# Expert stage of a two-layer MoE block: wide and narrow quads of experts alternate, and the hidden transpose moves to another PSUM bank

## The chip, the cores and the metric

The kernel runs on one core of one Trainium2 chip. The metric is device time in microseconds of one execution, lower is better; the time before is the median of three runs. A profile of one further execution, with its own time, is the source of every duration below.

## What is computed

The program takes 256 tokens of width 1024 through two layers of a mixer block with a dense feed-forward part, and then through two layers that end in a mixture of experts. The change touches only the latter. Of the reference, what matters is this:

```python
D_MODEL, SEQ, DEPTH = 1024, 256, 2
N_GROUPS, EXPERTS_PER_GROUP, N_EXPERTS, TOP_K, D_EXPERT = 4, 8, 32, 2, 512

def hierarchical_moe(h, w_group, b_group, w_router, b_router, w_gate, w_up, w_down):
    g_logits = xf @ w_group + b_group          # a token picks one group of 8 experts
    e_logits = xf @ w_router + b_router        # and its two best experts in that group
    ...
    def expert_block(args):
        xblk, e = args
        hid = jax.nn.silu(xblk @ w_gate[e]) * (xblk @ w_up[e])
        return hid @ w_down[e]
    ...                                        # weighted sum of the two experts of each token
```

All in fp32. An expert's three matrices are 2 MB each, so a layer's 32 experts are 201 MB that are read from HBM once. With 256 tokens and two experts each, an expert has 16 tokens on the mean. Evaluating this routing on the reference's inputs gives the largest number of tokens of one expert in each of the eight consecutive groups of four experts: 34, 35, 30, 20, 22, 26, 30, 18 in layer 0 and 15, 19, 29, 28, 18, 20, 19, 16 in layer 1.

## The kernel before

The expert stage is the function `moe` (L1530). It works on **quads** of four experts, `qd` = 0 to 7. A token's place in an expert's list is its slot. In a **wide** quad each expert has 64 slots and the quad is done in two steps of two experts; in a **narrow** quad each has 32 slots and the quad is one step of four experts. In both cases a step fills the 128 columns of the TensorE array, 64 or 32 columns for each expert (`tile_position` at L1600 and L1628), and matmuls of different columns run beside each other. So TensorE needs about twice the time for a wide quad, while the weights to be loaded are the same. `steps(qd)` (L86) says which it is: before, quads 0 to 3 are wide and 4 to 7 narrow (`NWIDE = 4`).

A quad's work, by the names that the profile shows:

- `prep` (L1566) picks the tokens: one-hot matrices `sel` on DVE (L1538), then `gather` (L1544), 32 matmuls `xt` (L1554) into PSUM pool `pX` of two banks, and evictions `XT` by DVE (L1558) and ACT (L1560). The matmuls are 256 columns for a wide quad and 128 for a narrow one; a wide quad needs four banks, a narrow one two. There is one `XT` buffer, so evictions wait until the previous quad's gate and up products are done.
- `up` (L1590) makes the gate product `g` and the up product `u` (L1600), each in one PSUM bank of its own (`pG`, `pU`), then `sl` = silu(g)·u on ACT (L1607) and DVE (L1608).
- `hidden` (L1611) turns `sl` by four transposes `hTp` (L1614) into a bank of `pX` and copies it back on ACT (L1616).
- `down` (L1619) makes the down product `yp` (L1628), `halves` (L1633) scales and splits it, `combine` (L1642) adds it to `x` by 8 matmuls `cb` (L1648). `combine` of a step runs inside `up` of the next one, after the gate product was issued.

Weights come through a **ring** of 10 buffers of 1 MB (class `Ring`, L186; the stage's pools have 3, 4 and 3 of them). The loads stand in one list, are issued by SP in order (L220), and a load is issued when its buffer comes free, which is after the last matmul that read it. An expert needs 6 loads: two halves each of gate, up and down; a quad needs 24.

Before quad 6 (`XAT = 6`) stands a branch (`overflow`, L1692, taken at L1698) for experts whose tokens exceed their slots. Its condition is `rv > over`: the largest count in `key`, from which `cm` was subtracted (L1515 to L1518), so that narrow experts count from 33 tokens and wide ones from 65. After quad 5 the stage combines, passes the branch and only then prepares quad 6.

The order of instructions on each engine is made by a scheduler from the program and its buffers; it moves the matmuls of `gather` between those of other steps where the banks of `pX` allow.

Of the kernel before, what the change touches and what calls it, by code (L numbers as in the profile page):

```python
# [11 lines left out]
F32 = mybir.dt.float32  # L12
# [8 lines left out]
P = 128  # L21
# [37 lines left out]
NE = 32  # L59
DE = 512  # L60
QE = 4
NWIDE = 4
XCAP = 64
KEY = 64
ALPHA = (2.0 * DEPTH) ** 0.25
# [19 lines left out]

def steps(qd):  # L86
    e = QE * qd
    return [(e, 2, 64), (e + 2, 2, 64)] if qd < NWIDE else [(e, 4, 32)]


def const_layout():
# [162 lines left out]
def v3(a, b):  # L254
    return lambda t: t[:, : a * b].rearrange("p (a b) -> p a b", a=a)


class Kern:
# [862 lines left out]
    def plan_second(self, i):  # L1121
# [18 lines left out]
        for qd in range(NE // QE):  # L1140
            if qd == NE // QE - 1:
                ring.blank()
            for e0, n, w in steps(qd):
                es = range(e0, e0 + n)
                for nm in ("e_w_gate_2", "e_w_up_2"):
                    for hf in range(2):
                        for e in es:
                            ring.add((ap[nm][i, e].rearrange("(p k) f -> p k f", p=P)[:, 4 * hf : 4 * hf + 4, :], v3(4, DE)))
                for hf in range(2):
                    for e in es:  # L1150
                        ring.add((ap["e_w_down_2"][i, e].rearrange("(p f) d -> p f d", p=P)[:, 2 * hf : 2 * hf + 2, :], v3(2, D)))
# [294 lines left out]
    def route(self, i, pool, pC, rw, csum, crow, stats, meanwhile):  # L1446
        nc = self.nc
        tmp = pool.tile([P, DE], F32, name="rt", tag="sl")
        used = [0]

        def tt(w):
            used[0] += w
            return tmp[:, used[0] - w : used[0]]

        U32 = mybir.dt.uint32
        A = pool.tile([P, NT, NE], BF16, name="Am")
        R, W = [pool.tile([P, NT, NE], F32, name=n) for n in ("R", "W")]
        key, cm = [pool.tile([P, NE], F32, name=n) for n in ("key", "cm")]
        k8 = pool.tile([P, 8], F32, name="k8")
        mi = pool.tile([P, 4], I32, name="mi")  # L1460
        hT = [pool.tile([P, D], F32, name=n, tag=n).rearrange("p (q k s) -> p q k s", q=2, k=4) for n in ("XT", "y")]
        self.nmr, late = [], []
        for t, ((mu, rs), bs) in enumerate(stats):
            for q, b in enumerate(bs):
                if EV[2 * t + q] == "v":
                    nc.vector.tensor_copy(hT[t][:, q], b)
                else:
                    with self.after(*([self.sq_last] if EV[2 * t + q] == "b" else [])):
                        nc.scalar.copy(hT[t][:, q], b)
            lg = pC.tile([P, 36], F32, name="lg", tag="c")  # L1470
            for k in range(KT):
                last = nc.tensor.matmul(lg, lhsT=hT[t][:, k // 4, k % 4, :], rhs=rw[:, k, :], start=k == 0, stop=k == KT - 1)
            nm = pool.tile([P, 1], F32, name="nmr", tag="nmr", bufs=2)
            self.nmr.append(nm)
            L = tt(36)
            nc.vector.tensor_tensor(nm, mu, rs, ALU.mult)
            nc.vector.scalar_tensor_tensor(L, csum, nm, crow, ALU.mult, ALU.add)
            nc.vector.scalar_tensor_tensor(L, lg, rs, L, ALU.mult, ALU.add)
            G, E = L[:, 0:4], L[:, 4:36]
            gm, t4, ix, ml, m8, xf, o1 = tt(1), tt(4), tt(1), tt(NE), tt(8), tt(2), tt(NE)  # L1480
            x8 = tt(8).bitcast(U32)
            nc.vector.tensor_reduce(gm, G, axis=AX.X, op=ALU.max)
            nc.vector.scalar_tensor_tensor(t4, G, gm, self.c("rev4"), ALU.is_equal, ALU.mult)
            nc.vector.tensor_reduce(ix, t4, axis=AX.X, op=ALU.max)
            nc.vector.tensor_scalar(t4, t4, ix, -1.0, op0=ALU.is_equal, op1=ALU.add)
            nc.vector.scalar_tensor_tensor(
                ml.rearrange("p (g e) -> p g e", g=4), t4.unsqueeze(2).to_broadcast([P, 4, 8]), -NEG,
                E.rearrange("p (g e) -> p g e", g=4), ALU.mult, ALU.add,
            )
            nc.vector.max(m8, ml)  # L1490
            nc.vector.max_index(x8, m8, ml)
            nc.vector.tensor_scalar(xf, x8[:, 0:2], -1.0, 32.0, op0=ALU.mult, op1=ALU.add)
            nc.vector.tensor_scalar(o1, self.c("rev32"), xf[:, 0:1], None, op0=ALU.is_equal)
            nc.vector.scalar_tensor_tensor(A[:, t, :], self.c("rev32"), xf[:, 1:2], o1, ALU.is_equal, ALU.add)
            late.append((G, gm, ml, m8, xf, t4))
        with self.after(last):
            meanwhile()
        rk = pC.tile([P, 3, NE], F32, name="rk", tag="c")
        nc.tensor.matmul(rk[:, 0, :], lhsT=self.strictb, rhs=A[:, 0, :], start=True, stop=False)
        nc.tensor.matmul(rk[:, 1:3, :], lhsT=self.onesb, rhs=A[:, 0, :].unsqueeze(1).to_broadcast([P, 2, NE]), start=False, stop=False)  # L1500
        nc.tensor.matmul(rk[:, 2, :], lhsT=self.onesb, rhs=A[:, 1, :], start=False, stop=False)
        nc.tensor.matmul(rk[:, 1, :], lhsT=self.strictb, rhs=A[:, 1, :], start=False, stop=True)
        r_last = nc.vector.scalar_tensor_tensor(R, rk[:, 0:2, :], 1.0, A, ALU.add, ALU.mult)

        def weights():
            for t, (G, gm, ml, m8, xf, t4) in enumerate(late):
                nc.vector.tensor_scalar(xf[:, 0:1], m8[:, 0:1], -1.0, None, op0=ALU.mult)
                nc.vector.tensor_scalar(xf[:, 1:2], gm, -1.0, None, op0=ALU.mult)
                nc.scalar.activation(ml, ml, AF.Exp, bias=xf[:, 0:1])
                nc.scalar.activation(t4, G, AF.Exp, bias=xf[:, 1:2], accum_out=gm)  # L1510
                nc.scalar.activation(m8[:, 1:2], m8[:, 1:2], AF.Exp, bias=xf[:, 0:1])
                nc.vector.scalar_tensor_tensor(gm, m8[:, 1:2], 1.0, gm, ALU.add, ALU.mult)
                nc.vector.reciprocal(gm, gm)
                nc.vector.scalar_tensor_tensor(W[:, t, :], ml, gm, A[:, t, :], ALU.mult, ALU.mult)
            nc.vector.memset(cm[:, : QE * NWIDE], 0.0)  # L1515
            nc.vector.memset(cm[:, QE * NWIDE :], float(32 - XCAP))
            nc.vector.tensor_tensor(key, rk[:, 2, :], cm, ALU.subtract)
            nc.vector.scalar_tensor_tensor(key, key, float(KEY), self.c("rev32"), ALU.mult, ALU.add)  # L1518
            nc.vector.max(k8, key)
            nc.vector.max_index(x8, k8, key)  # L1520
            nc.vector.tensor_copy(mi[:, 0:2], x8[:, 0:2])
            nc.vector.scalar_tensor_tensor(gx, k8[:, 0:1], float(-KEY * XCAP), k8[:, 2:3], ALU.add, ALU.max)
            nc.vector.tensor_copy(mi[:, 2:3], k8[:, 0:1])
            nc.vector.tensor_copy(mi[:, 3:4], gx)

        x8 = tt(8).bitcast(U32)
        gx = tt(1)
        return R, W, (key, cm, k8, mi), weights

    def moe(self, i, pool, A, B, R, W, g1, xs, weights, late, pG, pU, pY, pX, pC):  # L1530
        nc = self.nc
# [34 lines left out]
        def prep(qd, then=None):  # L1566
            w = steps(qd)[0][2]
            sel = slots(QE * w)
            last = pick(sel, QE, w, R, slice(QE * qd, QE * qd + QE))
            if then:  # L1570
                with self.after(last):
                    then()
            return gather(sel), sel
# [35 lines left out]
            return sl, last  # L1609

        def hidden(sl):  # L1611
            b = pX.tile([P, 4, P], F32, name="hTp", tag="x")
            for f in range(4):
                nc.tensor.transpose(b[:, f, :], sl[:, f::4], self.ident)  # L1614
            hid = v3(4, P)(sl)
            nc.scalar.copy(hid, b)  # L1616
            return hid
# [401 lines left out]
```

## Time and profile before

| | |
|---|---|
| median of 3 runs | 2090.56 us (2088.88 to 2095.25) |
| the profiled execution's own time | 2082.7 us |
| its span | 2080.5 us |
| TensorE busy, share of the span | 1869.5 us, 90% |
| mean DMA rate over the span | 288 GB/s |
| expert stage of layer 0, first gate matmul to last down matmul | 984.7 to 1455.2 us |
| expert stage of layer 1, likewise | 1591.7 to 2064.3 us |

A busy TensorE in these rows is not one at its peak, because matmuls overlap and their ends are modelled. The DMA share is the mean busy share of 16 DMA engines, and in the expert stage GB/s tells directly how fast weights arrive: 422 to 423 GB/s is the most that any longer stretch shows. PEclk is the granted TensorE clock, 1.00 being 2.4 GHz and 0.50 being 1.2 GHz.

### The profile page before, as it was taken

The numbers are of one execution on the slowest core, as the hardware profiler recorded it, in microseconds if no ns is written. First come the engines' busy times: TensorE is split into PE (matmuls) and PEld (weight loads), VectorE is DVE, ScalarE is ACT, GpSimd is POOL, SyncE is SP. The second block draws the span as 40 slices with busy tenths as digits, with TensorE's granted clock in tenths as the row PEclk, the third lists the DMA queues.
The fourth block names the chain that finished last, engine by engine and source line by source line (L and its number), as shares of the span: only waits on it lengthen the run. The fifth ranks groups of instructions, "written<-read, shape, count | busy, mean of one in ns | idle before, by whom it ended". The sixth has DMA issues, their size and how long they took to land. (4 is left out here: it accounts for less than half of the span.)

```text
span 2080.5 us, 27466 instructions
## 1 busy us (share of the span) xinstructions
PE 1869.5 (90%) x10924; PEld 1252.4 (60%) x10924; DVE 985.7 (47%) x1979; ACT 600.5 (29%) x1158; POOL 183.7 (9%) x219
## 2 busy tenths in 40 slices
PE   7999999999989999688999997687898999987775
PEld 7887899998879998666444432231895443331321
DVE  6556779574667786986222121110884222211112
ACT  5434534273445442324111110010443111010010
POOL 2210000021100001620200000000330200000000
PEclk9787999996889998798999999889898999999898
DMA  7232879451349796355899989999755999989996
GB/s 217 88 102 81 317 259 370 152 156 60 102 169 322 273 351 212 119 169 206 362 423 422 422 322 424 421 390 416 255 196 229 423 422 422 390 339 422 413 400 266
DMA packets 178252, 598.51 MB, mean 288 GB/s; under 512 B 19008, under 2 KB 105408, under 8 KB 128960
## 3 DMA queue, kind: packets, MB, share of 16 engines
q1 hardware_dynamic: 174912, 592.47, 74.3%
q10 hardware_dynamic: 1872, 2.26, 0.3%
q0 software_dynamic: 1328, 1.90, 0.3%
q8 instruction: 90, 1.47, 0.3%
q14 instruction: 50, 0.41, 0.1%
HBM read 594.66 MB, written 1.93 MB: 287 GB/s over the span
## 5 line engine op out<-in xcount | busy, mean ns | idle before, releaser
L378 DVE TENSOR_TENSOR wlo<-w,whi 128x1024 fp32r<-128x1024 f32 (+3 forms) x232 | 280.6, 1222 | 102.2 <-ACT whi L377 101.2
L377 ACT CAST whi<-w 128x1024 fp32r<-128x1024 f32 (+3 forms) x232 | 224.2, 983 | 229.0 <-PE gu L412 60.9
L1600 PE MATMUL g<-w,XT 128*64 128x512 f32 (+1 forms) x1024 | 240.4, 631 | 17.7 <-DMA w<-in_e_w_gate_dram 17.7
L1628 PE MATMUL yp<-w,sl 128*64 128x512 f32 (+1 forms) x1024 | 237.3, 631 | 17.8 <-DMA w<-in_e_w_down_dram 10.7
L1600 PE MATMUL u<-w,XT 128*64 128x512 f32 (+1 forms) x1024 | 215.3, 615 | 28.5 <-DMA w<-in_e_w_up_dram 28.5
L1638 DVE SCALAR_TENSOR_TENSOR y<-yp,ws,g 128x512 f32<-128x512 f32 x48 | 35.9, 749 | 293.7 <-PE yp L1628 286.9
L1608 DVE TENSOR_TENSOR sl<-sl,u 128x512 f32<-128x512 f32 x24 | 16.5, 687 | 312.6 <-PE u L1600 312.6
L1628 PEld LDWEIGHTS yp<-w,sl 128*64 128x64 f32 (+1 forms) x1024 | 69.9, 129 | 157.1 <-issue 113.2
L1600 PEld LDWEIGHTS u<-w,XT 128*64 128x64 f32 (+1 forms) x1024 | 61.8, 126 | 157.9 <-issue 108.7
L413 PE MATMUL gu<-hTf,wlo 128*128 128x256 f32 x512 | 147.0, 287 | 0.7 <-DVE wlo L378 0.6
L411 PE MATMUL gu<-hTf,whi 128*128 128x256 f32 x512 | 146.7, 287 | 0.8 <-ACT whi L377 0.8
L412 PE MATMUL gu<-hTf,whi 128*128 128x256 f32 x512 | 146.4, 286 | 0.0
L1600 PEld LDWEIGHTS g<-w,XT 128*64 128x64 f32 (+1 forms) x1024 | 63.0, 129 | 136.4 <-issue 100.6
L813 DVE SCALAR_TENSOR_TENSOR aacc<-w,ca,aacc 128x1024 f32<-128x1024 f32 x84 | 107.5, 1280 | 2.0 <-DMA w<-in_ada_w_dram 1.4
L399 ACT CAST yh<-y 128x512 fp32r<-128x512 f32 x48 | 29.7, 618 | 259.0 <-DVE y L1638 259.0
L411 PEld LDWEIGHTS gu<-hTf,whi 128*128 128x128 f32 x512 | 98.8, 193 | 2.7 <-ACT whi L377 1.0
L412 PEld LDWEIGHTS gu<-hTf,whi 128*128 128x128 f32 x512 | 99.4, 194 | 1.4
L413 PEld LDWEIGHTS gu<-hTf,wlo 128*128 128x128 f32 x512 | 98.7, 193 | 2.4 <-DVE wlo L378 1.1
L1554 PE MATMUL xt<-sel,nhh 128*128 128x256 f32 (+1 forms) x256 | 77.1, 328 | 22.5 <-DVE sel L1538 15.4
L1654 DVE TENSOR_TENSOR x<-x,cb 128x512 f32<-128x512 f32 x88 | 58.1, 685 | 79.5 <-PE cb L1648 79.3
L411 PE MATMUL mm<-whi,hT 128*128 128x384 f32 (+2 forms) x256 | 89.0, 355 | 4.6 <-ACT hT L495 4.6
L412 PE MATMUL mm<-wlo,hT 128*128 128x384 f32 (+2 forms) x256 | 89.8, 354 | 0.0
(476 smaller groups left out, 3697.8 us busy)
## 6 DMA issues: line engine op xcount, KB each, us to landing
w<-in_e_w_gate_dram SPq DMA_DIRECT2D x128, 1024.0 KB, 13.0
w<-in_e_w_down_dram SPq DMA_DIRECT2D x128, 1024.0 KB, 14.7
w<-in_e_w_up_dram SPq DMA_DIRECT2D x128, 1024.0 KB, 13.9
w<-in_ada_w_dram SPq DMA_DIRECT2D x48, 1024.0 KB, 7.7
w<-in_w_gate_dram SPq DMA_DIRECT2D x22, 1024.0 KB, 6.7
w<-in_w_up_dram SPq DMA_DIRECT2D x22, 1024.0 KB, 7.5
w<-in_w_down_dram SPq DMA_DIRECT2D x22, 1024.0 KB, 6.5
w<-in_w_in_dram SPq DMA_DIRECT2D x16, 768.0 KB, 4.4
```

The source lines that it names most:

```text
L377: self.half_act = nc.scalar.copy(hi, src)
L378: self.half_last = nc.vector.tensor_tensor(lo, src, hi.bitcast(F32), ALU.subtract)
L399: a = nc.scalar.copy(hi, src)
L411: nc.tensor.matmul(out, lhsT=a[0], rhs=b[0], start=start, stop=False)
L412: nc.tensor.matmul(out, lhsT=a[0], rhs=b[1], start=False, stop=False)
L413: self.mm_last = nc.tensor.matmul(out, lhsT=a[1], rhs=b[0], start=False, stop=stop)
L813: nc.vector.scalar_tensor_tensor(acc, w[:, j, :], c, acc, ALU.mult, ALU.add)
L1554: nc.tensor.matmul(b[:, k, :], lhsT=nh[hl][:, t, c0 : c0 + P], rhs=sel[:, t, :], start=t + hl == 0, stop=t + hl == NT)
L1600: last = nc.tensor.matmul(ps[c, :], lhsT=XT[:, kk, c], rhs=wt[j][:, k, :], start=kk == 0, stop=kk == KT - 1, tile_position=(0, w * j))
L1628: nc.tensor.matmul(ps[h][c, :], lhsT=hid[:, ff + f, c], rhs=wt[j][:, f, h * 512 : (h + 1) * 512], start=ff + f == 0, stop=ff + f == 3, til ...
L1638: nc.vector.scalar_tensor_tensor(y[:, c], ps[h], ws, g1[:, c], ALU.mult, ALU.mult)
L1654: nc.vector.tensor_tensor(a, a, b, ALU.add)
```

## The change

Quads 0, 1, 3 and 5 are wide now, and 2, 4, 6 and 7 narrow; there are four of each as before. `cm` is set by five memsets for two. The hidden transpose `hTp` takes the bank of the up product (`pU`, one bank) in place of one of the two of `pX`; the up product has been read by then, since `sl` is its last reader.

```diff
-NWIDE = 4
+WIDE = (0, 1, 3, 5)
...
 def steps(qd):
     e = QE * qd
-    return [(e, 2, 64), (e + 2, 2, 64)] if qd < NWIDE else [(e, 4, 32)]
+    return [(e, 2, 64), (e + 2, 2, 64)] if qd in WIDE else [(e, 4, 32)]
...
-            nc.vector.memset(cm[:, : QE * NWIDE], 0.0)
-            nc.vector.memset(cm[:, QE * NWIDE :], float(32 - XCAP))
+            nc.vector.memset(cm, float(32 - XCAP))
+            for qd in WIDE:
+                nc.vector.memset(cm[:, QE * qd : QE * qd + QE], 0.0)
...
         def hidden(sl):
-            b = pX.tile([P, 4, P], F32, name="hTp", tag="x")
+            b = pU.tile([P, 4, P], F32, name="hTp", tag="u")
```

In the changed program every line from L1516 on stands one lower, so `xt` is L1555, `hTp` L1615, `yp` L1629. How many gather matmuls `xt` the scheduler puts into each quad of a layer (from that quad's first `hTp` up to the next quad's): before, 32, 32, 32 and 64 in the wide quads 0 to 3 and none in the narrow quads 4 and 5; with the change 40 and 30 in quads 0 and 1, 48 in the narrow quad 2, 16 in the wide quad 3, 16 in the narrow quad 4 and none in the wide quad 5. The rest of quad 0's comes ahead of its first `hTp`.

TensorE before, second step of the wide quad 3 in layer 0 (`yp` is the down product, `w` the loaded weights; rows of the same kind are left out):

```order
L1614 MATMUL hTp<-ident,sl 128x128 x4
L1554 MATMUL xt<-sel,nhh 128x128
...
L1628 MATMUL yp_10888<-w_10685,sl 64x512
L1628 MATMUL yp_10888<-w_10687,sl 64x512
...
L1554 MATMUL xt<-sel,nhl 128x128
L1628 MATMUL yp_10888<-w_10699,sl 64x512
...
L1600 MATMUL g<-w_10731,XT 32x512
```

All 32 gather matmuls for quad 5 stand here, 16 between the transposes and the down product, 6 inside it and 10 after the next quad's first gate matmul.

TensorE with the change, the first step of the wide quad 3 in layer 0:

```order
L1615 MATMUL hTp<-ident,sl 128x128 x4
L1629 MATMUL yp_10677<-w_10550,sl 64x512
L1629 MATMUL yp_10678<-w_10550,sl 64x512
L1629 MATMUL yp_10677<-w_10552,sl 64x512
...
L1649 MATMUL cb<-yh,C 128x512
L1601 MATMUL g<-w_10574,XT 64x512
```

No gather stands in this step any more. Those for quads 3 and 4 have gone to the narrow quad 2, whose down product reads:

```order
L1615 MATMUL hTp<-ident,sl 128x128 x4
L1555 MATMUL xt<-sel,nhh 128x256
...
L1629 MATMUL yp_10532<-w_10363,sl 32x512
...
L1555 MATMUL xt<-sel,nhl 128x256
L1629 MATMUL yp_10532<-w_10367,sl 32x512
...
L1555 MATMUL xt<-sel,nhh 128x128
L1629 MATMUL yp_10532<-w_10369,sl 32x512
```

Here 48 gather matmuls stand between the 32 down matmuls.

ACT at the end of quad 3, before (`XT` is the gather's eviction, L1616 the copy that ends the use of the `hTp` bank):

```order
L1607 ACTIVATE sl<-g 128x512
L1560 ACTIVATE XT<-xt,B,A 128x128 x4
L1616 COPY sl<-hTp 128x512
L399 CAST yh<-y 128x512 x2
```

and with the change:

```order
L1608 ACTIVATE sl<-g 128x512
L1561 ACTIVATE XT<-xt,B,A 128x128 x2
L1617 COPY sl<-hTp 128x512
L1561 ACTIVATE XT<-xt,B,A 128x128 x2
```

The copy no longer stands behind all four evictions.

## Rows read from the trace of the kernel before

**Rows 1.** Page, parts 1 and 2: busy time; DMA share in 40 slices.

```profile
PE 1869.5 (90%) x10924; PEld 1252.4 (60%) x10924; DVE 985.7 (47%) x1979; ACT 600.5 (29%) x1158; POOL 183.7 (9%) x219
...
DMA  7232879451349796355899989999755999989996
```

**Rows 2.** Windows: length, busy by engine, PEclk, DMA share, GB/s.

```profile
1103.27:1195.00 91.73, 87.30 (x408) 36.73 (x406) 19.70 (x32) 9.98 (x21) 0.00 (x0) 0.98 1.01 422
1195.00:1255.00 60.00, 56.77 (x303) 21.86 (x303) 13.31 (x23) 6.74 (x15) 0.00 (x0) 0.94 0.85 336
1255.00:1345.00 90.00, 62.98 (x324) 18.75 (x314) 14.43 (x26) 6.28 (x13) 0.00 (x0) 0.90 1.01 423
1345.00:1375.00 30.00, 30.00 (x203) 15.34 (x205) 1.64 (x4) 2.86 (x7) 0.00 (x0) 0.80 0.91 364
...
1770.00:1865.00 95.00, 90.94 (x476) 36.16 (x476) 19.36 (x32) 9.58 (x21) 0.00 (x0) 0.98 0.91 358
...
1955.00:1985.00 30.00, 29.48 (x208) 15.28 (x207) 1.96 (x5) 2.86 (x7) 0.00 (x0) 0.84 0.90 364
```

**Rows 3.** DMA view, gate loads issued in 1110-1165, 1165-1245 and 1271-1330: us to landing.

```profile
w<-in_e_w_gate_dram SPq DMA_DIRECT2D x8, 1024.0 KB, 12.6
...
w<-in_e_w_gate_dram SPq DMA_DIRECT2D x8, 1024.0 KB, 7.4
...
w<-in_e_w_gate_dram SPq DMA_DIRECT2D x8, 1024.0 KB, 19.7
```

**Rows 4.** Waits of SP's queue, 1200 to 1255: us in total, times, longest.

```profile
SPq L220 <- PE g L1600: 22.7, 6, 9.5
SPq L220 <- PE yp L1628: 16.8, 3, 11.7
```

**Rows 5.** Groups by line, PE, quads 2 and 3 (1103.27 to 1235.12), and that window.

```profile
L1554 PE MATMUL xt<-sel,nhh 128*128 128x128 f32 (+1 forms) x43 | 12.3, 317 | 2.0 <-ACT XT L1560 2.0
L1554 PE MATMUL xt<-sel,nhl 128*128 128x128 f32 (+1 forms) x43 | 12.0, 309 | 0.0
...
L1614 PE MATMUL hTp<-ident,sl 128*128 128x128 f32 x16 | 3.3, 337 | 3.7 <-ACT XT L1560 2.7 <-DVE sl L1608 1.0
...
1103.27:1235.12 131.85, 124.50 (x557) 51.38 (x554) 28.39 (x48) 15.07 (x32) 0.00 (x0) 0.96 0.98 403
```

**Rows 6.** Timeline of PE at the end of quad 3 [idle before].

```profile
1209.65 7.04 PE L1600 MATMUL u<-w,XT 128*64 128x512 f32 x30
1219.35 0.75 PE L1614 MATMUL hTp<-ident,sl 128*128 128x128 f32 x4 [2.66 <-ACT XT L1560]
...
1222.68 6.04 PE L1628 MATMUL yp<-w,sl 128*64 128x512 f32 x16
...
1231.47 3.65 PE L1628 MATMUL yp<-w,sl 128*64 128x512 f32 x12
```

**Rows 7.** Windows of PE alone there: busy, PEclk, DMA share, GB/s.

```profile
1215.00:1220.00 5.00, 2.34 (x12) 1.00 1.01 426
1220.00:1225.00 5.00, 5.00 (x23) 0.57 1.02 428
1225.00:1230.00 5.00, 5.00 (x16) 0.75 0.24 85
```

**Rows 8.** Groups by line, PE, narrow quad 5 (1271.46 to 1331.96), and that window.

```profile
L1628 PE MATMUL yp<-w,sl 128*32 128x512 f32 x67 | 16.3, 600 | 3.0 <-DMA w<-in_e_w_down_dram 2.3 <-ACT sl L1616 0.7
L1600 PE MATMUL g<-w,XT 128*32 128x512 f32 x64 | 14.7, 732 | 3.3 <-DMA w<-in_e_w_gate_dram 3.3
L1600 PE MATMUL u<-w,XT 128*32 128x512 f32 x64 | 13.2, 642 | 6.2 <-DMA w<-in_e_w_up_dram 6.2
...
1271.46:1331.96 60.50, 45.90 (x226) 11.87 (x224) 6.36 (x11) 3.47 (x7) 0.00 (x0) 0.92 1.01 422
```

**Rows 9.** Waits of SP's queue at the branch, 1348 to 1369.

```profile
SPq L1698 <- SPq L1698: 19.4, 6, 5.3
```

**Rows 10.** Source view of L1515: one memset of `cm`, ns min/median/max.

```profile
L1515 DVE MEMSET cm<- x2: 72/72/72, 981.4 to 1588.4; 128x16 f32 x2
```

## The prediction

> **What bounds the kernel now.** I read the page first. TensorE is busy for 90% of the span and DMA is at nine tenths in most slices of the last half [rows 1], so the page alone doesn't say which of the two bounds the expert stage. The windows do. DMA moves 422 or 423 GB/s through nearly the whole stage: in quads 2 and 3 of layer 0 up to 1195 us, and again from 1255 us [rows 2]. That is the ceiling, since TensorE waits for loads in the second of these stretches and still gets no more [rows 8]. A quad is 24 loads of 1024 KB [rows 3], 25.17 MB, and takes 25.17 / 0.422 = 59.6 us at that rate. So the stage is bound by the loads, and time can be won only where DMA stops.
>
> It stops at two places in a layer. One is between 1195 and 1255 us, at 336 GB/s, which is where quad 3, the last wide one, hands over to quad 4; in layer 1 the like stretch is 1770 to 1865 us, at 358 GB/s [rows 2]. The other is at the branch after quad 5, 364 GB/s in 30 us in both layers [rows 2].
>
> Why the first? A load is issued when a ring buffer is free, so the time from issue to landing tells how many loads are queued; 10 buffers at 2.48 us each (59.6 / 24) make 24.8 us. For gate loads it is 12.6 us in quad 2's stretch, 7.4 us from 1165 us on, and 19.7 us in the narrow quad 5 [rows 3]. So the queue shrinks while wide quads run: TensorE frees buffers more slowly than DMA fills them, until DMA stops. What SP then waits for is TensorE, 22.7 us for gate and 16.8 us for down matmuls [rows 4]. TensorE's pace in quads 2 and 3 is 131.85 / 2 = 65.9 us a quad [rows 5] against 59.6. In quad 5 it has 45.9 us of busy time, waits for all three products' loads, and DMA is full [rows 8].
>
> **The change, part by part.** *The order of the quads.* The same four wide and four narrow quads run, so neither bytes nor matmuls change; what moves is the gather. Before, quad 3 alone has 64 gather matmuls and quads 4 and 5 have none. Now the wide quad 3 has 16, the wide quad 5 none and the narrow quad 2 has 48. In the two quads of rows 5 the gather's groups are busy for 12.3 + 12.0 = 24.3 us, and TensorE stands 2.0 us before `xt` and 2.7 us before `hTp`, each for evictions of `XT`. Without them the two quads are 131.85 - 29.0 = 102.9 us, 51.4 us a quad. I give quads 3 and 5 between 51.4 us and, with 16 gather matmuls at 24.3 / 86 = 0.28 us, 55.9 us. Both are under 59.6 us. Quads 0 and 1 keep their place and about their gather (70 matmuls for 64, some narrower), so they leave the queue as they did, at 12 us or more. Then the narrow quad 2 fills it up, quad 3 no longer empties it, and quad 4 and quad 5 repeat that. The stop at the hand-over goes: (422 - 336) / 422 x 60.00 = 12.2 us in layer 0 and (422 - 358) / 422 x 95.00 = 14.4 us in layer 1, **26.6 us** together. Since loads bound the rest of the stage, the end of it comes that much earlier, and what follows each stage hangs on its end.
>
> *The gather in quad 2.* 48 matmuls at 0.28 us are 13.4 us, put between down matmuls that are busy for 16.3 us [rows 8]. Together they are 29.7 us, where the eight down loads take 19.9. Quad 2 then ends up to 9.8 us late. Its cover is the queue: 24.8 us less the 7.4 us from issue to landing at which it ran dry, 17.4 us. So I cost it at nothing; with that cover gone, at 9.8 us a layer.
>
> *The transpose's bank.* Before, `hTp` at the end of quad 3 stood 2.66 us for the evictions, and the granted clock of the next windows was 0.57 and 0.75; 16 down matmuls there took 6.04 us, and 12 a little later 3.65 [rows 6, 7]. In `pU` it waits for `sl` only, and the copy no longer stands behind four evictions. That gain is in the 2.7 us above, and I don't count it twice. What is late next: the next up product needs the bank back. a whole gate product stands ahead of it on TensorE, so the copy is done by then, and I cost it at nothing; if it were not, TensorE would wait before every up product, and the loads' queue would cover that as well.
>
> *The branch.* SP stands 19.4 us at the branch [rows 9], for all loads in flight to land, before it issues another. That doesn't depend on the quads' widths, so (422 - 364) / 422 x 30.00 = 4.1 us a layer stays. If TensorE reached it far later, more would be lost; by the sum above quad 5 ends where its loads do, as now.
>
> *The memsets.* Three more, at 72 ns [rows 10], 0.2 us a layer if nothing hides them, in work that DVE does just ahead of the first gate matmul. 26.6 - 0.4 = 26.2; I take **26.5** off, with no more precision meant than 2 us.
>
> The profiled execution took 2082.7 us, so the sum gives 2056. The median of the runs shown is 2090.56, 8 us above it, and I forecast a median: 2090.56 - 26.5 = **2064 us**.
>
> **Rivals.** *Quad 2's gather is not absorbed* (place: its down product). For it: 29.7 us of TensorE work on 19.9 us of loads, and quads 0 and 1 may leave TensorE behind already. Against: 17.4 us of cover. Price 9.8 us a layer, 19.6 in all: 2064 + 19.6 = **2084 us**.
>
> *The hand-over itself stops DMA*, since a narrow step needs four experts' halves at once and keeps four buffers until all are used. For it: the stop in both layers lies just there, and SP waits for gate matmuls there [rows 4]. Against: the time from issue to landing fell through quad 3 already [rows 3]. There are now two more hand-overs ahead of quad 6, from quad 1 to 2 and from 5 to 6, and the branch hides the second. If only the one in the middle still costs, nothing is won: 2090 us; if that from quad 1 to 2 costs as much, 26.6 us more: 2117 us.
>
> *The clock falls in wide quads that wait for loads.* This is the rival on the other side. Wide quads now have gaps before loads as quad 5 had. At a granted clock of 0.50, 51.4 us at 0.96 become 98.7 us, 39.1 over the loads' 59.6; 17.4 of it the queue covers, and 21.7 are lost in each of quads 3 and 5, so 43.4 a layer against some 13.3 won: 30 us a layer slower, **2151 us**. It decides where two quads lose 13.3 us together, at an overrun of 24 us: a mean clock of 51.4 x 0.96 / 83.6 = 0.59. Against: quad 5, with waits before all three products, was granted 0.92 [rows 8], and at 0.92 a wide quad is 53.6 us.
>
> The Trainium skill, TensorE: Matmul & The Clock Gate, section "Why this matters for your kernels", speaks against the change: it wants the matmuls dense, and has a loop that waits for a transfer before each burst of matmuls run with the cold clock. By that rule the time would be this last rival's 2151 us. Rows 7 agree that the clock falls behind a stall; rows 8 show that waits of this kind before loads cost little of it.
>
> That a narrow quad's experts overflow, so that the branch is taken, is excluded: quads 2 and 4 have at most 30 and 22 tokens an expert.
>
> **How the numbers follow.** About 0.3%, 6.3 us, is what a measurement of this kernel can tell from no change. Forecast 78%: 2058 to 2072. Gather not absorbed, wholly or in part, 12%: up to 2084. Hand-over 6%, of it 4% without change and 2% slower. Clock 4%. So faster 0.90, same 0.04, slower 0.06. The range goes down to 2054: all 26.6 us, half of the 8.2 us at the branches, and the 6 us by which runs differ; and up to 2084, the first rival. Outside lie the 10% of the other two.
>
> **What would show it.** Right: in both layers 422 GB/s from the first freed buffers to the branch, with no dip where a wide quad ends; gate loads of quads 3 and 5 with about 19 us from issue to landing; TensorE waiting for loads inside wide quads; no wait of `hTp` for `XT`; the branch's 364 GB/s dip as it was. Wrong: a dip in quad 2 or 3 (gather), dips at quad 1 to 2 and 3 to 4 (hand-over), a clock under 0.8 in quads 3 and 5 (clock), or a full DMA rate with the end of the stage where it was.

## The result and the profile after

The changed kernel takes **2066.6 us**, the median of 4 runs (2065.01 to 2067.24). The kernel before takes 2089.72 beside it (2087.91 to 2095.25, 4 runs). The ratio is 0.9884 with a 95% interval of 0.9864 to 0.9904: the change made the kernel 23.1 us, 1.2%, faster. The forecast was 2064 us, with a range of 2054 to 2084.

The profiled execution of the changed kernel took 2067.24 us, with a span of 2065.0. First the page, parts 1 and 2, which answers to [rows 1]:

```profile
PE 1876.1 (91%) x10924; PEld 1251.1 (61%) x10924; DVE 981.7 (48%) x1985; ACT 599.7 (29%) x1158; POOL 186.5 (9%) x219
...
DMA  6232879552339798337699999999755999999996
```

TensorE has the same number of instructions and 6.6 us more busy time, in a span that is 15.5 us shorter. The digits of the DMA row show where the change is. In the kernel before, an 8 stood in each expert stage past its first slice, in those that begin at 1196 and 1820 us. Now every slice that lies wholly in one of the two stages is a 9.

The windows of the changed kernel (columns as in [rows 2]): quads 2, 3, 4 and 5 of layer 0, each from the last down matmul of the quad ahead to its own last one, then the branch of each layer.

```profile
1108.05:1149.99 41.94, 40.35 (x288) 17.88 (x288) 8.63 (x15) 4.89 (x10) 0.00 (x0) 1.00 1.01 422
1149.99:1214.63 64.64, 59.52 (x254) 22.53 (x254) 14.27 (x24) 7.12 (x17) 0.00 (x0) 0.97 1.01 423
1214.63:1266.67 52.04, 42.43 (x240) 12.70 (x240) 8.23 (x14) 5.50 (x11) 0.00 (x0) 0.93 1.01 422
1266.67:1327.49 60.82, 55.56 (x237) 20.27 (x236) 11.92 (x18) 5.61 (x12) 0.00 (x0) 1.00 1.01 423
1345.00:1375.00 30.00, 28.29 (x200) 13.40 (x199) 3.71 (x9) 4.09 (x11) 0.00 (x0) 0.88 0.89 359
...
1940.00:1970.00 30.00, 30.00 (x205) 14.92 (x205) 1.64 (x4) 2.86 (x7) 0.00 (x0) 0.84 0.90 362
```

DMA is at 422 or 423 GB/s in all four quads, where [rows 2] had 336 at the hand-over. The dip at the branch is as it was. The lengths tell why: the narrow quad 2 takes TensorE 41.94 us and the narrow quad 4 52.04, where the loads of a quad take 59.6. The wide quad 3 takes 64.64 and the wide quad 5 60.82. A wide quad falls behind the loads by 1 to 5 us, and the narrow one ahead of it has given more than that.

What SP waits for says the same. First the kernel before, in the wide quads 2 and 3 (1110 to 1195 us), then the changed kernel in quads 3 to 5 (1150 to 1330 us): us in total, times, longest.

```profile
SPq L220 <- PE yp L1628: 31.1, 6, 9.6
SPq L220 <- PE g L1600: 23.7, 9, 5.5
SPq L220 <- PE u L1600: 17.8, 8, 4.1
```

```profile
SPq L220 <- DMA w<-in_e_w_up_dram: 51.6, 24, 3.3
SPq L220 <- DMA w<-in_e_w_gate_dram: 50.0, 24, 2.1
SPq L220 <- DMA w<-in_e_w_down_dram: 49.7, 24, 2.1
SPq L220 <- PE yp L1629: 1.2, 4, 0.4
```

Before, SP waited for TensorE to free a buffer. Now it waits for other loads to land, 72 times, and for TensorE for next to nothing. The last four gate loads of quad 3 and the eight of quad 4, issued from 1146 to 1205 us, have 19.7 us to landing where the wide quads of [rows 3] had 12.6 and 7.4:

```profile
w<-in_e_w_gate_dram SPq DMA_DIRECT2D x12, 1024.0 KB, 19.7
```

**An account by landings.** Each load's record has the time at which it landed. A layer has 192 expert loads, counted here in the order in which they land, of 2.48 us each at the full rate, so a stretch can be told by how much later than that its loads land. I give three numbers a layer. A: from the first gate matmul to the landing of the 48th load, the last of quad 1. B: by how much the 96 loads of quads 2 to 5 land later than 238.1 us after it. C: by how much the last 48, with the branch, land later than 119.0 us after those. The sum with 238.1 and 119.0 is the stage from its first gate matmul to its last load. Layers 0 and 1, in us, from the profiled execution of each kernel:

| kernel | A | B | C | stage | median, us |
|---|---|---|---|---|---|
| before | 92.4, 92.9 | 13.1, 14.9 | 4.2, 4.1 | 466.8, 469.0 | 2089.7 |
| changed | 94.2, 95.5 | 1.2, 1.1 | 3.8, 4.1 | 456.3, 457.8 | 2066.6 |

The stages are 10.5 and 11.2 us shorter, 21.7 together. B gives 11.9 + 13.8 = 25.7, A takes 1.8 + 2.6 = 4.4 of it back, and C gives 0.4. The two profiled executions differ by less, 15.5 us, because that of the changed kernel began its first gate matmul 5.6 us later (990.3 for 984.7), after code that the change doesn't touch. Three executions of the changed kernel have this start at 984.0, 986.0 and 990.3, so executions differ by that much in any case.

### The profile page after: what moved, and what is told of

The parts are those of the page before. It is cut to its first block, busy times and chain, and to the rows that moved or that the text cites. A ratio compares the mean times of both kernels' runs of the same rounds, so it can differ in the third digit from the quotient of the medians.

```text
span 2065.0 us, 27481 instructions
## 1 busy us (share of the span) xinstructions
PE 1876.1 (91%) x10924; PEld 1251.1 (61%) x10924; DVE 981.7 (48%) x1985; ACT 599.7 (29%) x1158; POOL 186.5 (9%) x219
## 5 line engine op out<-in xcount | busy, mean ns | idle before, releaser
L378 DVE TENSOR_TENSOR wlo<-w,whi 128x1024 fp32r<-128x1024 f32 (+3 forms) x232 | 274.4, 1195 | 102.1 <-ACT whi L377 101.2
L1629 PE MATMUL yp<-w,sl 128*64 128x512 f32 (+1 forms) x1024 | 230.3, 599 | 19.2 <-DMA w<-in_e_w_down_dram 9.9
L1601 PE MATMUL u<-w,XT 128*64 128x512 f32 (+1 forms) x1024 | 221.0, 627 | 28.6 <-DMA w<-in_e_w_up_dram 28.5
L1601 PE MATMUL g<-w,XT 128*64 128x512 f32 (+1 forms) x1024 | 230.1, 630 | 8.5 <-DMA w<-in_e_w_gate_dram 8.5
L1629 PEld LDWEIGHTS yp<-w,sl 128*64 128x64 f32 (+1 forms) x1024 | 67.0, 123 | 149.5 <-issue 107.6
L399 ACT CAST yh<-y 128x512 fp32r<-128x512 f32 x48 | 29.7, 618 | 238.7 <-DVE y L1639 238.7
L1561 ACT ACTIVATE XT<-xt,B,A 128x256 f32<-128x256 f32 (+1 forms) x64 | 31.6, 515 | 206.8 <-DVE XT L1559 206.8
## 6 DMA issues: line engine op xcount, KB each, us to landing
w<-in_e_w_gate_dram SPq DMA_DIRECT2D x128, 1024.0 KB, 19.7
w<-in_e_w_up_dram SPq DMA_DIRECT2D x128, 1024.0 KB, 19.7
```

The lines of the kernel that those rows point to most:

```text
L378: self.half_last = nc.vector.tensor_tensor(lo, src, hi.bitcast(F32), ALU.subtract)
L399: a = nc.scalar.copy(hi, src)
L1561: nc.scalar.activation(XT[:, kk, :], b[:, k, :], AF.Identity, scale=A[:, kk : kk + 1], bias=B[:, kk : kk + 1])
L1601: last = nc.tensor.matmul(ps[c, :], lhsT=XT[:, kk, c], rhs=wt[j][:, k, :], start=kk == 0, stop=kk == KT - 1, tile_position=(0, w * j))
L1629: nc.tensor.matmul(ps[h][c, :], lhsT=hid[:, ff + f, c], rhs=wt[j][:, f, h * 512 : (h + 1) * 512], start=ff + f == 0, stop=ff + f == 3, til ...
```

## The experiments

**Theory.** The order wins: the narrow quads 2 and 4 fill the queue of loads before a wide quad draws on it, and nothing else counts. The bank costs a little in quads 0 and 1. **Rivals:** the bank wins, by taking the transposes off the evictions; or it is the hand-over, or strict alternation, that decides.

### The order alone, twice

```diff
-            b = pU.tile([P, 4, P], F32, name="hTp", tag="u")
+            b = pX.tile([P, 4, P], F32, name="hTp", tag="x")
```

> The changed kernel with the order of the quads alone: hTp stays in the xt bank. Theory (the order wins by keeping loads queued through quads 2 to 5; the bank only costs a little in quads 0 and 1, where the second step's up product now stands behind the first step's transposes): the middle of the stage loads without a stop as in the changed kernel, and the late landings of quads 0 and 1, 4.0 and 5.0 us a layer in the changed kernel, go back to about 2 us: 2062 us (2059 to 2066). Rival (the bank is what wins, the order follows along): no more than a third of the gain, 2082 us or above, with the stop near the end of quad 3 still there. Rival (both needed): some 2070 to 2076, with hTp waiting for XT's evictions in narrow quads.

Measured: **2063.83 us** (before beside it 2090.87; ratio 0.988, 0.986 to 0.99). A 92.8, 92.9; B 1.3, 1.1; C 4.2, 4.2. All of the gain in B is there without the bank, and A is back at what it was before the change. The rival that the bank wins falls, and with it the one that needs both: `hTp` still waits for evictions of `XT` here, 5.6 us in three places from 1093 to 1333 us, and the loads of quads 2 to 5 land as in the changed kernel.

This run also tells the order from the gather's new place. Without the bank the scheduler leaves most of the gather on the wide quad 3. Quads 2 and 3 of layer 0, cut as above, and then the gather's `xt` alone in quad 3 (busy time of PE, PEld, DVE and ACT, with no column for POOL):

```profile
1109.05:1145.63 36.58, 33.68 (x248) 13.62 (x248) 8.37 (x15) 4.61 (x10) 0.00 (x0) 0.95 1.01 422
1145.63:1215.60 69.97, 65.50 (x287) 26.79 (x288) 14.25 (x24) 7.60 (x17) 0.00 (x0) 0.98 1.01 423
...
1145.63:1215.60 69.97, 7.73 (x48) 6.71 (x48) 1.48 (x4) 1.61 (x4) 0.98 1.01 423
```

Quad 3 has 48 gather matmuls and takes 69.97 us, 10 more than its loads, and DMA stays at 423 GB/s. The narrow quad 2 ahead of it took 36.58, 23 less than its loads. So it is the narrow quad ahead of it that wins, and not that the gather has left quad 3, as it has in the changed kernel.

> The kernel with the order of the quads alone once more, now beside the changed kernel on the same chip. Theory (the bank costs 2 to 3 us a layer in quads 0 and 1 and gives nothing back): loads of quads 0 and 1 late by 2 us a layer, those of quads 2 to 5 by 1 to 2, and a median 4 us under the changed kernel's. Rival (the bank's cost there is taken back in quads 2 to 5): the same median within 1 us.

Measured: 2067.29 us (ratio 0.9883, 0.9865 to 0.9901), A 92.2, 92.9, B 1.6, 1.1. The landings agree with the theory again. The median doesn't: it lies 1.5 us above that of the changed kernel beside it, and the theory wanted 4 below.

### The bank alone

```diff
-WIDE = (0, 1, 3, 5)
+WIDE = (0, 1, 2, 3)
```

> The kernel before with hTp in the up product's bank alone: quads 0 to 3 wide, then 4 narrow. Theory (order wins): the stop at the hand-over stays for the most part; the wait of hTp for XT (2.7 us in two quads of layer 0) goes, and quads 0 and 1 lose 2 to 3 us a layer of landings: between 2084 and 2092 us. Rival (the bank wins): 2066 to 2072 us, no stop between 1195 and 1255 us.

Measured: **2095.5 us**, ratio to before 1.002 (1.0006 to 1.0033), so slower, and 3.5 us above the range that I gave. A 94.2, 94.9; B 12.9, 16.7. The windows of quads 2 to 5, from 100 us after the first gate matmul of each layer, for the bank alone (columns as in [rows 2]):

```profile
1091.65:1331.65 240.00, 211.87 (x1071) 79.42 (x1070) 48.16 (x81) 24.96 (x55) 0.00 (x0) 1.00 0.98 400
1703.91:1943.91 240.00, 215.43 (x1072) 80.14 (x1072) 48.96 (x82) 25.73 (x57) 0.00 (x0) 0.98 0.97 395
```

And the like windows of the changed kernel:

```profile
1090.34:1330.34 240.00, 217.31 (x1101) 81.10 (x1100) 51.73 (x87) 26.39 (x57) 0.00 (x0) 0.98 1.01 423
1686.90:1926.90 240.00, 217.96 (x1116) 81.36 (x1113) 51.36 (x87) 27.60 (x59) 0.00 (x0) 0.99 1.01 421
```

400 and 395 GB/s against 423 and 421, and 401 and 397 in the like windows of the kernel before: with the bank and the old order the stop stays whole. That `hTp` no longer waits for `XT` won nothing, although that wait was in the trace before.

### The changed kernel again, twice

> The changed kernel itself, unchanged, beside the other kernels of this call on the same chip. Both theories: 2066 to 2069 us. If it comes out at 2071 us or above, the 2073 and 2072 us of the kernels with wide quads 0, 1, 4, 5 and with 0, 1 alone lie within what this chip's executions differ by, and nothing is to be read from their medians against 2066.6 us.

Measured: 2068.71 us (2061.21 to 2075.35), A 94.0, 95.0, B 1.4, 1.2. That is under the 2071 us that I had set, so this run doesn't put the 2073 and 2072 us of the two kernels below down to scatter.

> The changed kernel once more, as the measure for the other three of this call: loads of quads 0 and 1 late by 4 to 5 us a layer by the theory; by the rival that the first two measurements of this stretch were chance, anything between 2 and 5.

Measured: 2065.76 us, A 94.2, 95.1, B 1.3, 1.4. In three executions A is 94.0 to 95.5 with the bank. In the two with the order alone and in that of before it is 92.2 to 92.9. The bank's cost in quads 0 and 1 is no chance, though its 17th to 48th loads are late by 3.5 to 5.0 us, a little less than I wrote.

### Where wide quads follow one another

Two in a row, after two narrow ones:

```diff
-WIDE = (0, 1, 3, 5)
+WIDE = (0, 1, 4, 5)
```

> Wide quads 0, 1, 4, 5: two wide ones in a row after two narrow ones, nothing else changed. Theory (what counts is that the queue is full when wide quads begin, and that TensorE's lag over two of them stays under the 17 us of cover): no stop, 2066 us (2064 to 2069), issue to landing of gate loads falls in quad 5 from 20 to 8-14 us. Rival (wide and narrow must alternate; the pair itself stops DMA as quads 2 and 3 did): a stop of some 5 to 13 us a layer near quad 5's end, 2076 to 2090 us.

Measured: 2073.19 us (2069.66 to 2075.85; ratio to before 0.9918, 0.9903 to 0.9934). A 94.8, 95.2; B 1.1, 2.5; C 4.0, 5.0; stage 457.1, 459.9. There is no stop near quad 5's end, so the rival of strict alternation falls. Half of my expectation fell too: the time to landing didn't sink in quad 5, where it is 19.9 us. Quads 4 and 5, in this kernel both wide:

```profile
1205.70:1268.09 62.39, 57.95 (x254) 22.38 (x254) 14.20 (x22) 7.76 (x17) 0.00 (x0) 1.00 1.01 422
1268.09:1326.19 58.10, 53.87 (x237) 21.10 (x234) 12.09 (x18) 6.22 (x13) 0.00 (x0) 1.00 1.01 423
```

With 16 gather matmuls in it a wide quad falls behind by 2.8 us; the next one, with none ahead of the branch, wins 1.5 back. So a wide quad draws the queue down by what gather it has: in the profiles of all the kernels here the wide quads from 2 on took 56.3 to 61.1 us without any, and 66.2 to 71.6 with 36 or more, in layers 0 and 1. Before, quads 2 and 3 had 32 and 54 in each layer, cut the same way, and nothing narrow between them. The median is 6.6 us above the changed kernel's first one, and the stages account for 2.9 of that.

Three in a row, from the start:

```diff
-WIDE = (0, 1, 3, 5)
+WIDE = (0, 1, 2, 5)
```

> Wide quads 0, 1, 2, 5 instead of 0, 1, 3, 5: three wide ones in a row at the start, then two narrow ones. Theory (the queue is drawn down quad by quad while wide quads follow one another from the start, and DMA stops once it is gone): two in a row stopped nothing in the changed kernel and four in a row cost 13 to 17 us a layer in the kernel with the bank alone, so three leave a stop of 2 to 6 us a layer, ahead of the narrow quad 3: 2070 to 2078 us. Rival (one hand-over costs the same wherever it lies): 9 us or more a layer there, 2085 us or above. Rival (only the fourth wide quad in a row does harm): none, 2067 us.

Measured: **2084.74 us** (2070.97 to 2087.37; ratio to before 0.9959, 0.9941 to 0.9977). A 94.2, 95.4; B 6.9, 7.6; C 4.6, 4.6. The stop lies in the loads of quad 3, as the theory has it, but is 7 us a layer where I gave 2 to 6, and the median lies 6.7 us above my range. The time is near the rival's 2085, but that rival wants a like stop at the first hand-over of the changed kernel, from quad 1 to 2, and its 24 loads after that land 0.2 us early and 0.3 late. Two wide quads from the start cost nothing, three 7 us a layer, four 13 to 17. What SP waits for there, 1135 to 1190 us, is TensorE again:

```profile
SPq L220 <- PE yp L1629: 23.6, 6, 8.2
SPq L220 <- PE g L1601: 10.9, 3, 6.6
SPq L220 <- PE u L1601: 5.5, 3, 2.6
```

Only quads 0 and 1 wide:

```diff
-WIDE = (0, 1, 3, 5)
+WIDE = (0, 1)
```

> Only quads 0 and 1 wide, the other six narrow: the same loads, less TensorE work from quad 2 on. Theory (from quad 2 on the changed kernel is bound by the loads alone): the same time as the changed kernel, 2066 us (2063 to 2068). Rival (wide quads 3 and 5 still cost something by themselves, in TensorE's time or clock): 2055 to 2061 us.

Measured: 2072.44 us (2067.56 to 2077.32; ratio to before 0.9918, 0.9898 to 0.9937), and 2067.56 in the profiled execution, 0.3 above the changed kernel's. A 94.2, 94.5; B 1.5, 2.6; stage 457.0, 459.0. With two wide quads fewer the stage is no shorter. So quads 3 and 5 cost nothing in the changed kernel by being wide, and what bounds it from quad 2 on is the loads. The median misses my range by 4 us; the stages account for 1.9.

### The branch taken away

```diff
-                self.overflow(i, pool, A, B, R, W, g1, xs, pG, pU, pY, pX, pC, (pick, gather, slots, turn, up, hidden, down, halves, combine))
```

> The changed kernel without the branch for overflowing experts ahead of quad 6, so that this path is left out; the gather for quad 6 stays where it is. Theory (the loads bound the stage, and SP's drain ahead of the branch costs them 4 us a layer): 8 us less than the changed kernel, 2058 us (2056 to 2061), and the loads of quads 6 and 7 land within 0.5 us of the full rate. Rival (what stood behind the branch is lost anyway, in TensorE's gather ahead of quad 6): less than 3 us, 2064 us or above.

Measured: **2058.99 us** (2051.1 to 2063.92; ratio to before 0.984, 0.9812 to 0.9868), 9.7 below the changed kernel beside it. C is 0.0, 1.3 for 3.8, 4.1; the stages are 452.4, 455.1, so 3.9 and 2.7 shorter. The window with quad 6's start in each layer shows no dip:

```profile
1330.00:1375.00 45.00, 39.48 (x217) 12.22 (x219) 8.13 (x17) 4.26 (x10) 0.00 (x0) 0.92 1.01 423
1930.00:1975.00 45.00, 37.78 (x207) 11.41 (x209) 7.45 (x13) 4.26 (x10) 0.00 (x0) 0.89 1.01 423
```

The price of the branch, 4.1 us a layer, was read rightly from its dip, though layer 1 gave a little less than that back: its last 48 loads are 1.3 us late where I gave 0.5.

### What the bank does in quads 0 and 1

The bank only from quad 2 on:

```diff
-        def hidden(sl):
-            b = pU.tile([P, 4, P], F32, name="hTp", tag="u")
+        def hidden(sl, own=False):
+            b = pX.tile([P, 4, P], F32, name="hTp", tag="x") if own else pU.tile([P, 4, P], F32, name="hTp", tag="u")
...
-                pend = (C, halves(down(hidden(sl), n, w, take, self.ring.done), ws))
+                pend = (C, halves(down(hidden(sl, qd < 2), n, w, take, self.ring.done), ws))
```

> The changed kernel with hTp in the xt bank for quads 0 and 1 and in the up product's bank from quad 2 on. Theory (the up product's bank costs 2 to 3 us a layer in quads 0 and 1 and nothing later): the late landings of quads 0 and 1 go from 4.0 and 5.0 back to 2 us, 4 to 5 us less than the changed kernel beside it, like the kernel with the order alone: 2062 to 2064 us. Rival (the bank costs in quads 2 to 5 too, or not at all): as the changed kernel, 2066 to 2068 us, or with late landings from quad 2 on.

Measured: 2069.12 us (ratio to before 0.9894, 0.987 to 0.9918). A 92.5, 93.1; B 1.4, 1.3; stage 455.2, 455.5. By the landings the theory holds: A is back and nothing is lost later. By the median it can't be told from the changed kernel beside it, 2068.71, and it lies 5 us above the range that I gave.

What changes there stands in TensorE's timeline. The second step of quad 0, in the kernel before (start, us, instruction):

```profile
1012.75 2.31 PE L1600 MATMUL u<-w,XT 128*64 128x512 f32 x9
...
1015.61 7.07 PE L1628 MATMUL yp<-w,sl 128*64 128x512 f32 x32
1022.51 5.32 PE L1600 MATMUL u<-w,XT 128*64 128x512 f32 x22
```

And in the changed kernel:

```profile
1021.99 7.07 PE L1629 MATMUL yp<-w,sl 128*64 128x512 f32 x32
1028.88 5.31 PE L1601 MATMUL u<-w,XT 128*64 128x512 f32 x22
1034.12 0.51 PE L1649 MATMUL cb<-yh,C 128*128 128x512 f32 x1
```

Before, 10 up matmuls of the second step ran ahead of the first step's down product. The first two up buffers are read by 16, so they came free soon after it: the two loads that waited for them were issued 38.9 and 39.7 us after the first gate matmul. Now all of them stand behind the down product, and those two loads are issued at 42.2 and 42.6. Also, 10 matmuls of quad 1's gather stand ahead of the first step's transposes now. In the 100 us from the first gate matmul, what SP waits for shifts. Before:

```profile
SPq L220 <- PE g L1600: 47.2, 11, 13.1
SPq L220 <- PE yp L1628: 18.2, 6, 4.9
SPq L220 <- PE u L1600: 12.7, 10, 3.0
```

In the changed kernel:

```profile
SPq L220 <- PE g L1601: 36.7, 13, 8.5
SPq L220 <- PE yp L1629: 25.8, 7, 11.4
SPq L220 <- PE u L1601: 19.5, 11, 4.1
```

To tell the shared bank from the moved gather, the two were given other numbers of banks:

```diff
-            pU = s2.enter_context(tc.tile_pool(name=f"pU{i}", bufs=1, space=PSUM, reuse_waits="tile"))
+            pU = s2.enter_context(tc.tile_pool(name=f"pU{i}", bufs=2, space=PSUM, reuse_waits="tile"))
...
-            pX = s2.enter_context(tc.tile_pool(name=f"pX{i}", bufs=2, space=PSUM, reuse_waits="tile"))
+            pX = s2.enter_context(tc.tile_pool(name=f"pX{i}", bufs=1, space=PSUM, reuse_waits="tile"))
```

> The changed kernel with two banks for the up product and hTp and one for xt, instead of one and two. Theory (in quads 0 and 1 the second step's up product stands behind the first step's transposes because they share one bank): loads of quads 0 and 1 late by 2 to 3 us a layer instead of 4 to 5; the gather, with one bank, waits for each eviction, some 8 x 0.7 us a quad more on TensorE, which the queue covers: 2062 to 2066 us. Rival (it is the gather of quad 1, which now starts ahead of the first transposes, that delays the loads): still 4 us or more late there, and 2070 us or above with the slower gather.

Measured: 2072.52 us (ratio to before 0.9909, 0.9891 to 0.9927). The 17th to 48th loads are late by 2.8 and 2.2 us, as the theory wanted, but the 17th itself lands 16.4 and 16.3 us after the first gate matmul, where it was 13.3 and 13.7. A is 96.1, 95.4, no better, and the median lies 6.5 us above the theory's range, in that of the rival. The slower gather may have eaten what the bank gave. This run doesn't tell the two apart, and which part of the bank's move costs the 2 us stays open.

### Fewer buffers

```diff
-RING3 = 3
+RING3 = 1
```

> The changed kernel with 8 ring buffers in the expert stage instead of 10. Theory (quad 2's overrun of at most 9.8 us is covered by the buffers, and 8 of them, 19.8 us of loads, still cover it): loads of quads 2 to 5 late by under 3 us a layer; quads 0 and 1 lose the two loads that were ahead at the start and the two buffers of play, 5 to 8 us a layer: 2076 to 2086 us. Rival (the changed order has little cover to spare): stops of 5 us a layer or more in quads 2 to 5 as well, 2090 us or above.

The 8 and 10 here are wrong. Six buffers of an earlier pool (`ring1`, L1056) stay in the ring to the end of the program, so the edit takes it from 16 buffers to 14. The loads show it, those issued before the first gate matmul of layer 0, in the changed kernel and in this one (all have landed by then):

```profile
w<-in_e_w_gate_dram SPq DMA_DIRECT2D x8, 1024.0 KB, 7.4
w<-in_e_w_down_dram SPq DMA_DIRECT2D x4, 1024.0 KB, 9.0
w<-in_e_w_up_dram SPq DMA_DIRECT2D x4, 1024.0 KB, 8.4
...
w<-in_e_w_gate_dram SPq DMA_DIRECT2D x6, 1024.0 KB, 6.7
w<-in_e_w_down_dram SPq DMA_DIRECT2D x4, 1024.0 KB, 8.6
w<-in_e_w_up_dram SPq DMA_DIRECT2D x4, 1024.0 KB, 8.1
```

Measured: 2084.48 us (2076.79 to 2088.65; ratio to before 0.997, 0.9956 to 0.9985). A 98.8, 97.9; B 3.5, 2.5, of it 3.4 and 2.1 in the loads of quad 2; C 7.0, 5.0. B is at most 0.5 us over what I gave, and the rival's 5 us aren't there. From quad 3 on there is no stop with 14 buffers either, so what the narrow quad 2 gives is cover enough with two fewer. How few would do isn't shown. Quads 0 and 1 lost 4.6 and 2.4 us instead of 5 to 8, and the branch 1 to 3 that I hadn't expected. The landings account for 10.1 + 4.7 = 14.8 us of the 18.7 by which the median lies above the changed kernel's beside it.

**Is there a better kernel?** The order alone and the bank from quad 2 on have stages that are 1 to 2.6 us a layer shorter than the changed kernel's. Their medians, 2063.8, 2067.3 and 2069.1, don't stand apart from its 2066.6, 2068.7 and 2065.8. No run shows a version that does all of its work and beats it.

## Why the prediction was right, point by point

**The bound.** Right. Where SP waits for landings, DMA stays at 422 GB/s, and with two wide quads fewer the stage isn't shorter.

**The order of the quads.** Right, and nearly in size: 26.6 us forecast from the two GB/s windows, 25.7 measured in B, all of it from the order alone. The forecast gave the gather's move a part in it, since quad 3 was to have 16 gather matmuls. With 48 on quad 3, in the order alone, the gain is the same. That the old stop was a lag built up over wide quads, and not the hand-over, is shown by the doses: two, three and four wide quads from the start give 0, 7 and 13 to 17 us a layer.

**The pace of wide quads.** Too low. I gave 51.4 to 55.9 us of TensorE work, both under the loads' 59.6. Quad 5 was busy 55.56 us, in 60.82, and quad 3 was busy 59.52 us, in 64.64. So quad 3 does fall behind, by 5 us, and the forecast held because quad 2 is ahead by 17.7. The error is a sum. In [rows 5] the `nhh` and `nhl` matmuls of the gather alternate and overlap, and I added the busy times of the two groups, 12.3 + 12.0 = 24.3 us. Taken together they are busy for 13.69 us in quads 2 and 3 before (a view of `xt` alone, columns as in the one above for the order alone):

```profile
1103.27:1235.12 131.85, 13.69 (x86) 12.21 (x86) 3.56 (x8) 3.76 (x8) 0.96 0.98 403
```

With that a gather matmul is 0.16 us and not 0.28, and the two wide quads without gather and its waits are 131.85 - 13.69 - 4.7 = 113.5 us, 56.7 a quad, or 59.3 with 16 gather matmuls. TensorE's groups in quad 3, in a view by shapes:

```profile
L1601 PE MATMUL g<-w,XT 128*64 128x512 f32 x64 | 17.8, 599 | 0.0
L1629 PE MATMUL yp<-w,sl 128*64 128x512 f32 x64 | 17.5, 619 | 1.6 <-ACT sl L1617 1.6
L1601 PE MATMUL u<-w,XT 128*64 128x512 f32 x64 | 14.9, 592 | 0.0
...
L1555 PE MATMUL xt<-sel,nhh 128*128 128x256 f32 x8 | 2.7, 355 | 0.0
```

It waits for no load there, against what I said would show. In quad 5 its up product does, by 1.4 us:

```profile
L1601 PE MATMUL u<-w,XT 128*64 128x512 f32 x64 | 16.2, 596 | 1.4 <-DMA w<-in_e_w_up_dram 1.4
```

**The gather in quad 2.** Costed at nothing, and it cost nothing: the loads of quads 2 and 3 land within 0.3 us of the full rate. The 9.8 us of overrun come from the same double count. From the end of the up product to the last down matmul quad 2 took 21.04 us and not 29.7. All 48 gather matmuls and the 64 rows of the down product lie in it, the first busy for 6.65 us where I had 13.4, the second for 13.00 where I had 16.3 (views of `xt` and of `yp` alone; the second has no ACT):

```profile
1128.95:1149.99 21.04, 6.65 (x48) 5.82 (x48) 2.08 (x4) 2.27 (x4) 1.00 1.01 422
1128.95:1149.99 21.04, 13.00 (x64) 3.03 (x64) 0.75 (x1) 1.00 1.01 422
```

**The cover.** I took the ring for 10 buffers and a full queue for 24.8 us. The ring has 16, and the time to landing stops at 19.8 us with 16 buffers and with 14, since no more than eight loads are in flight. So my 17.4 us of cover was a number read from the wrong scale, and that the cost came out at nothing isn't owed to it. What the runs show is that 10 us of lag in quad 3 were covered (the order alone).

**The bank.** This step failed: "Quads 0 and 1 keep their place and about their gather (70 matmuls for 64, some narrower), so they leave the queue as they did". They left it 1.8 and 2.6 us later. I had asked whether the copy would be done in time for the next up product, and not what TensorE's new order frees later: the first two up buffers of quad 0's second step come free 3 us later. These 4.4 us are most of what the stages fell short of the forecast: 26.5 - 21.7 = 4.8. By the median the forecast missed by 2.6 us. The 2.7 us wait of `hTp` in the sum's evidence was no gain of its own, as the bank alone shows: it left 29.6 us of late landings in B, before 28.0.

**The branch and the memsets.** Right: 4 us a layer stay, and without the branch they go. The memsets of a layer now take 85 + 4 x 62 ns for 2 x 72, 0.2 us more.

**The rivals.** Gather not absorbed: no dip in quads 2 and 3. The hand-over: no dip from quad 1 to 2 nor from 3 to 4. The clock: quads 3 and 5 were granted 0.97 and 1.00, and quad 4, which waited 8.0 us for loads, 0.93; the rival needed a mean under 0.59. The rule in the Trainium skill, TensorE: Matmul & The Clock Gate, section "Why this matters for your kernels", which would have made it 2151 us, isn't borne out for waits of this size. Its loop has a long wait in it, and TensorE's longest wait for a load in quads 3 to 5 of layer 0 was 1.4 us; no run here has wide quads that wait for much longer.

## What to carry to other kernels

Where a stage streams weights and its steps differ in pace, look at what the issuing queue waits for. If it is an engine in one part and landings in another, the total can be balanced and the order still wrong: here, with fast steps put between the slow ones, nothing stopped. When groups of instructions overlap, take their busy time together and don't add the rows. And when a tile is moved to another bank, compare the order of instructions on the engine that fills it: what a buffer's release now stands behind can cost more than the wait that the move removes.

## What the runs showed that I had not expected

**Eight loads in flight, whatever the ring.** In quads 3 to 5 of the changed kernel each load is issued 0.06 us (0.39 in one case) after the eighth load before it landed, in all 72. The program uses eight semaphores in turn to tell of landings, and each of the 72 loads waits for its own, which the eighth load before it had. So the time to landing stays at 8 x 2.48 = 19.8 us with a ring of 16 buffers. With 14, SP's waits from 1150 to 1330 us look the same:

```profile
SPq L220 <- DMA w<-in_e_w_up_dram: 50.2, 24, 2.2
SPq L220 <- DMA w<-in_e_w_down_dram: 50.0, 24, 2.1
SPq L220 <- DMA w<-in_e_w_gate_dram: 48.4, 24, 2.1
```

So the time from issue to landing tells how near a queue is to running dry, but not how much stands behind it once it is at 19.7 us. This is also why it didn't sink in quad 5 of the kernel with wide quads 0, 1, 4, 5.

**A removed wait that cost time.** The bank alone made the kernel 0.2% slower (0.06 to 0.33%), though it took away a wait that the trace before shows.
